# First modulation vectors of a diffusion step: weights as the stationary operand, the two conditions as moving columns

## Chip, cores and metric

The kernel runs on one core of one Trainium2 chip. Its time is the device time of one execution in microseconds (us); less is better.

## What is computed

The reference is one inference step of a two-layer backbone for two request groups, 1,024 latent tokens and 128 prompt tokens of width 1,024, in float32. In each layer a condition vector gives six modulation vectors, which scale, shift and gate the tokens' normed values. Only the first two of layer 0, the shift and the scale ahead of its first mixer, are touched here:

```python
def ada_modulation(cond, w_ada, b_ada):
    m = jax.nn.silu(cond) @ w_ada + b_ada
    return jnp.split(m[:, None, :], N_ADA, axis=-1)

def modulate(x, norm_w, shift, scale):
    return rms_norm(x, norm_w) * (1 + scale) + shift
...
sh1_p, sc1_p, g1_p, ... = ada_modulation(c_ctx[None, :], ada_w[i], ada_b[i])
sh1_s, sc1_s, g1_s, ... = ada_modulation(c, ada_w[i], ada_b[i])
hp = modulate(xp, norm_mix[i], sh1_p, sc1_p)
hs = modulate(xs, norm_mix[i], sh1_s, sc1_s)
```

There are two conditions, one for each group. For these two vectors the product is [2 x 1024] by [1024 x 2048], that is 8 MB of float32 weights for 2 rows of data. What follows them is the projection of the modulated tokens with `win0`.

## The kernel before, in words

Activations lie transposed: channels on the 128 partitions, tokens along the free axis, 1,152 tokens in three chunks of 384. `x` is eight tiles (KD = 8) of 128 channels each. A modulation vector is wanted the same way, as a column of 128 channels for each of 8 tiles and 2 conditions; it is kept in `ada`.

The opening (lines 505 to 524) runs so. The program loads chunk 0 of `x` and takes its norm (`norm_stats`, L260): ACT squares eight tiles, DVE adds the even ones and POOL the odd ones (L271), DVE joins the two (L272), a matmul with `ones` (L274) sums over channels, and `rsqrt` (L251) follows on DVE and ACT. Then come `ada_mat(1)` (scale) and `ada_mat(0)` (shift), then four weight tiles of `win0`, each split into a high and a low part (`wsplit`, L156: ACT L160, DVE L161), then for each chunk `norm_apply` (L278): DVE multiplies by the scale (`ht`, L289), ACT adds the shift and rounds (`hh`, L290 and L292), DVE forms the remainder (`hl`, L294 and L296). The projection (`mm3`, L330) multiplies with three matmuls for each weight tile (L335 to L337) and is the first large product. A small transpose of the conditions (`ps_sil`, L519) and a cast of `sel8` (L517) for later stages stand at the end of the opening.

`ada_mat` for one part loads eight tiles of 128 x 1,024 weights (512 KB each), tile k holding input channels 128k to 128k + 127. For each it makes two products: the stationary operand is `sil`, 128 channels by 2 conditions; the moving operand is 512 columns of the weights. The result is two rows of 1,024. ACT copies them out of PSUM (`arow`, L228), eight transposes turn them into columns (L231), and `ada_bias` (L207) adds the bias on DVE (L210) and, for the scale, joins it with the norm's weights (L214).

Buffers of `S` (L55) are handed out by age: the slot that has been free longest comes first. `x`, the norm's buffer `nt`, the weight tiles `wadan`, `arow`, `hh`, `hl` and `ht` all take theirs from it, so an `nt` or `ht` often gets a slot in which a weight tile lay, and has to wait until TensorE has read that tile. In the kernel before, `nt` of chunk 1 gets the slot of the third tile of part 0, and `nt` of chunk 2 that of the eighth.

The order on each engine isn't that of the text: a scheduler of the language places the instructions of all engines by its own estimate of their times, and each engine then runs its own list strictly in order. All loads are issued on SP's queue.

Of the kernel before, what the change touches and what calls it, by code (L numbers as in the profile page):

```python
# [17 lines left out]
P = 128  # L18
D = 1024
KD = 8  # L20
# [70 lines left out]
def hybrid_kernel(ctx: ExitStack, tc: tile.TileContext, I, O):  # L91
    nc = tc.nc
# [7 lines left out]
    S = Slots(spool, NSLOT)  # L100
# [5 lines left out]
    def PS(name, tag="pa"):  # L106
        return psum.tile([P, 512], F32, tag=tag, name=name, bufs={"pa": 3, "pb": 3, "pc": 2}[tag])
# [4 lines left out]
    def dma(out, in_):  # L112
        nc.sync.dma_start(out.bitcast(F32) if out.dtype == F32R else out,
                          in_.bitcast(F32) if in_.dtype == F32R else in_)
# [27 lines left out]
    ident = cst.tile([P, P], F32, name="ident")  # L142
# [13 lines left out]
    def wsplit(src, e=0):  # L156
        r = W("wr")
        dma(r, src)
        hi, lo = W("wh"), W("wl")
        nc.scalar.copy(hi, r)  # L160
        (nc.gpsimd if e else nc.vector).tensor_sub(lo, r, hi)  # L161
        return hi, lo

    def wtile(w, n=8, width=P):
        return [(w[0][:, k * width:(k + 1) * width], w[1][:, k * width:(k + 1) * width]) for k in range(n)]
# [5 lines left out]
    sil = cst.tile([P, 2 * KD], F32, name="sil")  # L171
# [35 lines left out]
    def ada_bias(layer, part, src):  # L207
        a = ada[layer][:, 8 * part:8 * part + 8, :]
        b0 = VEC[f"bada{layer}"][0] + 8 * part
        nc.vector.tensor_add(a, src, vec[:, b0:b0 + 8].unsqueeze(2).to_broadcast([P, 8, 2]))  # L210
        if part in (1, 4):
            n0 = VEC[("nmix" if part == 1 else "nmlp") + str(layer)][0]
            nb = vec[:, n0:n0 + 8].unsqueeze(2).to_broadcast([P, 8, 2])
            nc.vector.scalar_tensor_tensor(a, a, 1.0, nb, op0=ALU.add, op1=ALU.mult)  # L214

    def ada_mat(part):
        ps = [PS("ps_a", "pc") for _ in range(2)]
        for k in range(KD):
            r = S.alloc("wadan")
            dma(r[:, :D], I["wada0"][part, k])  # L220
            for q in range(2):
                nc.tensor.matmul(ps[q][0:2], sil[:, 2 * k:2 * k + 2], r[:, q * 512:q * 512 + 512],
                                 start=k == 0, stop=k == KD - 1)
            S.free(r)
            yield
        row = S.alloc("arow")
        for q in range(2):
            nc.scalar.copy(row[0:2, q * 512:q * 512 + 512], ps[q][0:2])  # L228
        pt = PS("ps_at", "pb")
        for k in range(KD):  # L230
            nc.tensor.transpose(pt[:, 2 * k:2 * k + 2], row[0:2, k * P:k * P + P], ident[0:2, 0:2])  # L231
        S.free(row)
        ada_bias(0, part, pt[:, 0:16].rearrange("p (k i) -> p k i", i=2))
        yield

    bg = []
# [268 lines left out]
    load_x(0)  # L505
    stats = [norm_stats(x, 0)]
    run(ada_mat(1))
    run(ada_mat(0))
    ws = [wtile(wsplit(I["win0"][4 + g])) for g in range(4)]
    hh, hl = alloc_h()  # L510
# [7 lines left out]
    pt = PS("ps_sil", "pb")  # L518
# [22 lines left out]
    for ch in range(NCH):  # L541
        c0 = ch * CH
        for g in range(4):
            ps = PS("ps_i")[:, :CH]
# [72 lines left out]
    for m in (2, 3, 0, 1):  # L617
        w = wtile(wsplit(I["win0"][m]))
        for ch in range(NCH):
            ps = PS("ps_i")[:, :CH]  # L620
# [83 lines left out]
    for ch in range(NCH + 1):  # L704
# [4 lines left out]
        for t in range(4):  # L709
            ps = PS("ps_k")[:, :n]  # L710
# [464 lines left out]
    r, vr = S.alloc("ctx"), S.alloc("ctxv")  # L1175
# [20 lines left out]
    for g in range(4):  # L1196
# [8 lines left out]
        for t, ch in order:  # L1205
# [3 lines left out]
            ps = PS("ps_n1")[:, :CH]  # L1209
# [9 lines left out]
        for ch in range(NCH):  # L1219
            for t in range(4):  # L1220
                wn = "naq" if t < 2 else "nak"
                pp_ = pq if t < 2 else pk
                ps = PS("ps_b", "pb")[:, :CH]
# [230 lines left out]
def tile_w(w, cols=None):  # L1454
    k, m = w.shape
    return np.ascontiguousarray(w.reshape(k // P, P, m // P, P).transpose(2, 1, 0, 3)).reshape(m // P, P, k)


def layout(a):
    r = {}  # L1460
# [4 lines left out]
    def put(name, v):  # L1465
        o, w = VEC[name]
        vec[:, o:o + w] = v
# [3 lines left out]
    for i in range(2):  # L1471
        put(f"bada{i}", cols(a[f"b_ada_l{i}"]))
        put(f"nmix{i}", cols(a[f"norm_mix_l{i}"]))
        put(f"nmlp{i}", cols(a[f"norm_mlp_l{i}"]))
        w = np.asarray(a[f"w_ada_l{i}"])
        if i == 0:
            r["wada0"] = np.ascontiguousarray(w[:, :2 * D].reshape(KD, P, 2, D).transpose(2, 0, 1, 3))
            r["wada0t"] = np.ascontiguousarray(w[:, 2 * D:].T).reshape(32, P, D)
        else:
            r["wada1"] = np.ascontiguousarray(w.T).reshape(48, P, D)  # L1480
        r[f"w1_{i}"] = tile_w(a[f"w_mlp1_l{i}"])
        w2 = np.asarray(a[f"w_mlp2_l{i}"]).reshape(2, 8, 2, P, 4, 256)
        r[f"w2_{i}"] = np.ascontiguousarray(w2.transpose(1, 4, 3, 2, 0, 5)).reshape(8, 4, P, 1024)
# [5 lines left out]
    w = np.asarray(a["w_in_l0"])  # L1489
# [3 lines left out]
    w = np.asarray(a["w_q_up_l0"]).reshape(256, 8, 96)  # L1493
    r["wqup"] = np.concatenate([w[:, :, :64].reshape(256, 512), w[:, :, 64:].reshape(256, 256),
                                w[:, :, 64:][:, :, swap].reshape(256, 256)], axis=1).reshape(2, P, 1024)
    w = np.asarray(a["w_kv_up_l0"]).reshape(P, 8, 128)
    r["wkvup"] = np.concatenate([w[:, :, :64].reshape(P, 512), w[:, :, 64:].reshape(P, 512)], axis=1)
    w = np.asarray(a["w_pool_l0"]).transpose(1, 0, 2).reshape(P, 512)
    r["wpool"] = np.concatenate([w, np.zeros_like(w)], axis=1)
    for i in range(2):  # L1500
        w = np.asarray(a[f"w_out_l{i}"]).reshape(2, 4, P, 4, 2, P)
# [29 lines left out]
    for g in range(4):  # L1531
        w, h = 2 << g, 1 << g
        e[g, :h] = w / (np.arange(h) + h)
        e[g, 16 - h:] = w / np.minimum(np.arange(h, 0, -1) + h, w)
    w = np.asarray(a["w_in_l1"])
# [49 lines left out]
```

## Time and profile before

| | us |
|---|---|
| median of 3 runs (3025.92 to 3040.58) | 3026.92 |
| the profiled execution, device time | 3023.98 |
| its span in the profile | 3022.2 |
| first product of `ada_mat` starts | 11.92 |
| first matmul of the projection starts | 47.43 |

The profile is of one execution. Times in its rows are microseconds from the span's start; L222 is line 222 of the kernel. PE is TensorE's matmul, PEld its weight load (they overlap), DVE, ACT and POOL are the vector, scalar and GpSimd engines, SPq is the queue that issues loads. `out<-in` names the tiles, the number after x counts the records, and brackets give the idle time before them and what ended it. A form such as `128*2 128x512` is that of the array (rows by columns of the stationary operand) and of the data. The granted clock (PEclk) is 1.00 at full speed.

### The profile page before, as it was taken

The page shows a single profiled execution, that of the slowest core. Times are in us where ns is not written, and L with a number is a line of the kernel's source. Part 1 is how long each engine was busy: PE and PEld are TensorE (multiplying, and loading weights), DVE is VectorE, ACT ScalarE, POOL GpSimd, SP SyncE. Part 2 cuts the span into 40 slices and gives each one's busy share as a digit, 9 for nine tenths or more (in the row PEclk, how much of TensorE's full clock was granted, in tenths as well). Part 3 has the DMA queues.
Part 4 walks back from the last instruction along what each step waited for, and adds up shares of the span by engine and source line. Part 5 has one row for each costly group of instructions (what it writes and reads, how often), then busy time and mean ns, then how long its engine had stood idle before and what let it go on. Part 6 is the DMA issues. An engine that isn't in the chain of part 4 may idle for free.

```text
span 3022.2 us, 46490 instructions
## 1 busy us (share of the span) xinstructions
PE 2910.4 (96%) x18302; PEld 2611.2 (86%) x18302; DVE 2160.5 (71%) x3921; ACT 1330.5 (44%) x2177; POOL 312.7 (10%) x210
## 2 busy tenths in 40 slices
PE   7998999889999999999999999998989999999999
PEld 4956666689999999999988888665889999999999
DVE  5977343797668889777789533677687678777765
ACT  5364344243436543453634522443244355453432
POOL 2004000143000020000221000000030000110000
PEclk9996999999999999999999999998999999999999
DMA  6529331432322334322556537796303232332322
GB/s 234 168 64 318 86 77 44 129 119 77 101 81 92 105 119 154 91 84 84 171 162 214 178 129 194 198 240 165 108 28 99 78 98 84 116 99 78 98 78 87
DMA packets 148268, 372.37 MB, mean 123 GB/s; under 512 B 14225, under 2 KB 67073, under 8 KB 148050
## 3 DMA queue, kind: packets, MB, share of 16 engines
q1 hardware_dynamic: 148050, 369.40, 40.0%
q8 instruction: 144, 2.36, 0.3%
q14 instruction: 74, 0.61, 0.1%
HBM read 310.69 MB, written 57.47 MB: 122 GB/s over the span
## 4 chain that ended last, share of the span: by engine, by line
PE 84%; DVE 6%; DMA 6%; issue 2%; ACT 1%; POOL 1%; SPq 0%; DVEq 0%; POOLq 0%; ACTq 0%
PE ps L452 9%; PE ps L454 9%; PE ps L453 9%; PE ps L422 8%; PE ps L424 8%; PE ps L423 8%; PE ps_pv L1077 4%; PE ps_n L335 2%; PE ps_n L336 2%; PE ps_n L337 2%; DVE trash L200 1%; PE ps_pv L1330 1%; PE ps_v L1354 1%; PE ps_v L1356 1%; PE ps_v L1355 1%
## 5 line engine op out<-in xcount | busy, mean ns | idle before, releaser
L452 PE MATMUL ps<-ml,wh 128*128 128x288 f32 x2048 | 591.9, 295 | 10.3 <-DVE ml L441 7.8
L453 PE MATMUL ps<-mh,wl 128*128 128x288 f32 x2048 | 600.8, 295 | 0.0
L454 PE MATMUL ps<-mh,wh 128*128 128x288 f32 x2048 | 596.6, 295 | 0.0
L422 PE MATMUL ps<-bl,wh 128*128 128x288 f32 x1792 | 532.9, 298 | 13.4 <-DVE bl L353 10.2
L423 PE MATMUL ps<-bh,wl 128*128 128x288 f32 x1792 | 529.7, 296 | 0.0
L424 PE MATMUL ps<-bh,wh 128*128 128x288 f32 x1792 | 528.2, 295 | 0.0
L452 PEld LDWEIGHTS ps<-ml,wh 128*128 128x128 f32 x2048 | 381.2, 188 | 11.3 <-DVE ml L441 8.3
L453 PEld LDWEIGHTS ps<-mh,wl 128*128 128x128 f32 x2048 | 385.1, 188 | 0.0
L454 PEld LDWEIGHTS ps<-mh,wh 128*128 128x128 f32 x2048 | 383.2, 188 | 0.1
L458 DVE SCALAR_TENSOR_TENSOR x<-ps,ada,x 128x288 f32<-128x288 f32 (+2 forms) x640 | 270.1, 451 | 119.1 <-PE ps L454 117.6
L422 PEld LDWEIGHTS ps<-bl,wh 128*128 128x128 f32 x1792 | 336.9, 188 | 16.7 <-issue 11.5
L424 PEld LDWEIGHTS ps<-bh,wh 128*128 128x128 f32 x1792 | 338.4, 189 | 0.0
L423 PEld LDWEIGHTS ps<-bh,wl 128*128 128x128 f32 x1792 | 337.6, 188 | 0.2
L395 ACT CAST wh<-s 128x512 fp32r<-128x512 f32 x256 | 146.1, 618 | 307.0 <-PE ps L454 216.7
L160 ACT CAST wh<-wr 128x1024 fp32r<-128x1024 f32 x188 | 196.9, 1049 | 165.7 <-PE ps L424 79.9
L200 DVE CUSTOM_DVE_ANT_0 trash<-wada,silu 128x1024 bf16<-128x1024 f32 x160 | 217.1, 1357 | 18.2 <-DMA wada<-in_wada 7.6
L161 DVE TENSOR_TENSOR wl<-wr,wh 128x1024 fp32r<-128x1024 f32 x144 | 179.6, 1251 | 44.3 <-ACT wh L160 44.3
L395 ACT CAST wh<-wr 128x1024 fp32r<-128x1024 f32 (+1 forms) x128 | 107.0, 836 | 220.0 <-PE ps L454 155.5
L161 POOL TENSOR_TENSOR wl<-wr,wh 128x1024 fp32r<-128x1024 f32 x44 | 122.2, 2784 | 708.7 <-ACT wh L160 687.4
L1035 DVE TENSOR_REDUCE stat<-ps_m 128x1 f32<-128x384 f32 x192 | 98.3, 552 | 117.0 <-PE ps_m L1034 116.7
L396 DVE TENSOR_TENSOR wl<-s,wh 128x512 fp32r<-128x512 f32 x232 | 157.6, 711 | 5.1 <-ACT wh L395 2.8
L1279 DVE CUSTOM_DVE_ANT_0 trash<-ps_m,ta 128x512 bf16<-128x512 f32 (+1 forms) x128 | 83.5, 652 | 98.1 <-PE ps_m L1277 90.4
(315 smaller groups left out, 6113.8 us busy)
## 6 DMA issues: line engine op xcount, KB each, us to landing
wr<-in_w SPq DMA_DIRECT2D x256, 512.0 KB
wada<-in_wada SPq DMA_DIRECT2D x48, 512.0 KB
wada<-in_wada0t SPq DMA_DIRECT2D x32, 512.0 KB
wr<-in_win SPq DMA_DIRECT2D x24, 512.0 KB
wr<-in_wout SPq DMA_DIRECT2D x24, 512.0 KB
vd<-vst SPq DMA_DIRECT2D x27, 384.0 KB
kk<-kd SPq DMA_DIRECT2D x32, 288.0 KB
nv<-vd SPq DMA_DIRECT2D x16, 576.0 KB
```

The costliest lines, as they stand in the source:

```text
L160: nc.scalar.copy(hi, r)
L161: (nc.gpsimd if e else nc.vector).tensor_sub(lo, r, hi)
L200: nc.vector.tensor_tensor_reduce(trash, r[:, :D], silu[i][:, :D], scale=1.0, scalar=0.0, op0=ALU.mult, op1=ALU.add, accum_out=a)
L395: nc.scalar.copy(h, src)
L396: (nc.gpsimd if j in EDGE and min(ps) in EDGE_POOL else nc.vector).tensor_sub(l, src, h)
L422: nc.tensor.matmul(ps, wh[:, a], hl[:, b], start=k == 0, stop=False)
L423: nc.tensor.matmul(ps, wl[:, a], hh[:, b], start=False, stop=False)
L424: nc.tensor.matmul(ps, wh[:, a], hh[:, b], start=False, stop=k == 3)
L452: nc.tensor.matmul(ps, wh, hl, start=kk == 0, stop=False)
L453: nc.tensor.matmul(ps, wl, hh, start=False, stop=False)
L454: nc.tensor.matmul(ps, wh, hh, start=False, stop=kk == 3)
L458: nc.vector.scalar_tensor_tensor(x[m][:, a:b], ps[:, a - ch * HC:b - ch * HC], g, x[m][:, a:b], op0=ALU.mult, op1=ALU.add)
```

## The change

The operands of the product swap their places. The weights are stored in another order: tile m of a part now holds output channels 128m to 128m + 127, and within it eight blocks of 128 input channels by 128 output channels. Each block is a stationary operand, and the two columns of `sil` for its input channels are the moving operand. Eight such products add up to two columns of the result, which stand in PSUM as they are wanted. The copies to `arow` and the transposes fall away, and `ada_bias` reads PSUM directly. The number, size and order of the loads stay the same.

```diff
     def ada_mat(part):
-        ps = [PS("ps_a", "pc") for _ in range(2)]
-        for k in range(KD):
+        ps = PS("ps_a", "pc")
+        for m in range(KD):
             r = S.alloc("wadan")
-            dma(r[:, :D], I["wada0"][part, k])
-            for q in range(2):
-                nc.tensor.matmul(ps[q][0:2], sil[:, 2 * k:2 * k + 2], r[:, q * 512:q * 512 + 512],
+            dma(r[:, :D], I["wada0"][part, m])
+            for k in range(KD):
+                nc.tensor.matmul(ps[:, 2 * m:2 * m + 2], r[:, k * P:k * P + P], sil[:, 2 * k:2 * k + 2],
                                  start=k == 0, stop=k == KD - 1)
             S.free(r)
             yield
-        row = S.alloc("arow")
-        for q in range(2):
-            nc.scalar.copy(row[0:2, q * 512:q * 512 + 512], ps[q][0:2])
-        pt = PS("ps_at", "pb")
-        for k in range(KD):
-            nc.tensor.transpose(pt[:, 2 * k:2 * k + 2], row[0:2, k * P:k * P + P], ident[0:2, 0:2])
-        S.free(row)
-        ada_bias(0, part, pt[:, 0:16].rearrange("p (k i) -> p k i", i=2))
+        ada_bias(0, part, ps[:, 0:16].rearrange("p (k i) -> p k i", i=2))
         yield
...
-            r["wada0"] = np.ascontiguousarray(w[:, :2 * D].reshape(KD, P, 2, D).transpose(2, 0, 1, 3))
+            r["wada0"] = np.ascontiguousarray(w[:, :2 * D].reshape(KD, P, 2, KD, P).transpose(2, 3, 1, 0, 4)).reshape(2, KD, P, D)
```

From line 225 on the changed kernel's lines are seven lower (L267 there is L274 here, L328 is L335). With `arow` gone, the slots move on: `nt` of chunk 1 now gets the slot of the second tile of part 0, and `nt` of chunk 2 that of the seventh. The scheduler also places the work around the product otherwise. Three places show it.

On TensorE, where the product ends and the projection begins, the kernel before has (`wadan_42` is the last weight tile, `ps_n_336` the norm of chunk 1):

```order
L222 MATMUL ps_a_187<-wadan_42_217,sil_83 2x512
L222 MATMUL ps_a_188<-wadan_42_217,sil_83 2x512
L231 MATMUL ps_at_224<-ident_75,arow_44_221 128x2 x8
L274 MATMUL ps_n_336<-nt_71_314,ones_74 128x384
L335 MATMUL ps_i_501<-hl0_54_266,wh_236 128x384
L336 MATMUL ps_i_501<-hh0_46_258,wl_237 128x384
L337 MATMUL ps_i_501<-hh0_46_258,wh_236 128x384
```

The changed kernel has there (`ps_n_406` and `ps_n_476` are the norms of chunks 1 and 2):

```order
L222 MATMUL ps_a_222<-sil_83,wadan_38_283 128x2 x8
L222 MATMUL ps_a_222<-sil_83,wadan_40_293 128x2 x8
L267 MATMUL ps_n_406<-nt_67_384,ones_74 128x384
L267 MATMUL ps_n_476<-nt_77_454,ones_74 128x384
L512 MATMUL ps_sil_543<-ident_75,sil_83 16x128
L328 MATMUL ps_i_571<-hl0_50_336,wh_306 128x384
L329 MATMUL ps_i_571<-hh0_42_328,wl_307 128x384
```

The norm of chunk 2 and the small transpose, which stood some 80 rows further on, inside the projection, now stand ahead of its first matmul.

On DVE, around the addition of the bias to the shift (L210), the kernel before has (`nt_71` is chunk 1's norm, `nt_81` chunk 2's):

```order
L271 TENSOR_TENSOR nt_71_314<-nt_71_314,sq_329 128x384
L210 TENSOR_TENSOR ada0_91<-ps_at_224,vec_73 128x16
L272 TENSOR_TENSOR nt_71_314<-nt_71_314 128x384
L271 TENSOR_TENSOR nt_81_384<-nt_81_384,sq_387 128x384
L294 SCALAR_TENSOR_TENSOR hl0_54_266<-ht_62_274,ada0_91,hh0_46_258 128x384
L252 TENSOR_SCALAR nt_71_314<-ps_n_336 128x384
```

The changed kernel has there (`nt_67` is chunk 1's norm, `nt_77` chunk 2's):

```order
L265 TENSOR_TENSOR nt_67_384<-nt_67_384 128x384
L264 TENSOR_TENSOR nt_77_454<-nt_77_454,sq_457 128x384
L264 TENSOR_TENSOR nt_77_454<-nt_77_454,sq_463 128x384
L264 TENSOR_TENSOR nt_77_454<-nt_77_454,sq_469 128x384
L210 TENSOR_TENSOR ada0_91<-ps_a_222,vec_73 128x16
L265 TENSOR_TENSOR nt_77_454<-nt_77_454 128x384
L287 SCALAR_TENSOR_TENSOR hl0_50_336<-ht_58_344,ada0_91,hh0_42_328 128x384
```

The whole addition for chunk 2, which takes in POOL's half at L265, now stands ahead of the first `hl`.

On ACT, after the casts of the first `win0` tiles, the kernel before has:

```order
L160 CAST wh_248<-wr_246 128x1024
L267 ACTIVATE nt_71_314<-x0_1_93 128x384
L267 ACTIVATE nt_71_314<-x1_2_94 128x384
L270 ACTIVATE sq_317<-x2_3_95 128x384
L270 ACTIVATE sq_320<-x3_4_96 128x384
```

The changed kernel has there:

```order
L160 CAST wh_318<-wr_316 128x1024
L263 ACTIVATE sq_387<-x2_3_95 128x384
L263 ACTIVATE sq_390<-x3_4_96 128x384
L263 ACTIVATE sq_393<-x4_5_97 128x384
L263 ACTIVATE sq_396<-x5_6_98 128x384
L263 ACTIVATE sq_399<-x6_7_99 128x384
L510 CAST sel8r_77<-sel8_76 128x48
L260 ACTIVATE nt_67_384<-x0_1_93 128x384
L260 ACTIVATE nt_67_384<-x1_2_94 128x384
```

The first two squares of chunk 1, which go into `nt` itself, moved behind five others and behind the cast of `sel8`, which stood far behind them before.

## The prediction

> **What bounds the kernel now.** The page comes first: its span, its busy times and its chain.
>
> ```profile
> span 3022.2 us, 46490 instructions
> ...
> PE 2910.4 (96%) x18302; PEld 2611.2 (86%) x18302; DVE 2160.5 (71%) x3921; ACT 1330.5 (44%) x2177; POOL 312.7 (10%) x210
> ...
> PE 84%; DVE 6%; DMA 6%; issue 2%; ACT 1%; POOL 1%; SPq 0%; DVEq 0%; POOLq 0%; ACTq 0%
> ```
>
> TensorE is on 84% of the chain that ended last, so time that is added on TensorE is kernel time wherever TensorE does not wait afterwards. The change touches only the opening; the second view is therefore busy time by stretch (columns: busy us and instructions of PE, PEld, DVE, ACT, POOL, then granted clock, DMA share, GB/s).
>
> ```profile
> 11.92:15.94 4.02, 4.02 (x5) 0.84 (x6) 0.56 (x1) 0.00 (x0) 0.33 (x1) 1.00 1.02 419
> 15.94:43.20 27.26, 27.26 (x70) 5.49 (x68) 10.92 (x18) 9.43 (x16) 4.54 (x3) 1.00 1.04 392
> 43.20:46.66 3.46, 1.04 (x10) 0.87 (x10) 2.55 (x5) 3.38 (x8) 2.43 (x3) 1.00 0.90 365
> 46.66:50.08 3.42, 3.42 (x10) 2.75 (x10) 2.86 (x7) 3.42 (x8) 0.00 (x0) 0.50 0.04 12
> ...
> 67.40:155.00 87.60, 87.60 (x493) 85.74 (x494) 81.61 (x171) 36.79 (x81) 1.06 (x1) 1.00 0.49 155
> 155.00:225.00 70.00, 70.00 (x285) 38.04 (x284) 49.37 (x102) 48.07 (x111) 4.03 (x2) 1.00 0.18 56
> 225.00:268.00 43.00, 32.50 (x97) 24.22 (x97) 34.30 (x68) 18.16 (x20) 33.72 (x21) 0.53 0.88 329
> ```
>
> From 11.92 to 43.2 us TensorE never idles: the modulation product owns it. From 67.4 to 225 us it never idles either (87.60 of 87.60, 70.00 of 70.00). Whatever delays the first input projection is therefore carried through to 225 us unshortened. Then come waits (32.50 of 43.00).
>
> The third view is the opening in order of time, which gives the hand-over to the projection (L335).
>
> ```profile
> 11.92 3.57 PE L222 MATMUL ps_a<-wadan,sil 128*2 128x512 f32 x4 [11.92 <-DMA wadan<-in_wada]
> ...
> 15.43 1.15 PE L274 MATMUL ps_n<-nt,ones 128*128 128x384 f32 x2
> ...
> 16.51 12.18 PE L222 MATMUL ps_a<-wadan,sil 128*2 128x512 f32 x28
> ...
> 36.44 0.94 ACT L267 ACTIVATE nt<-x 128x384 f32<-128x384 f32 x2 [0.53 <-PE ps_a L222]
> ...
> 44.32 0.41 PE L231 MATMUL ps_at<-ident,arow 2*128 2x2 f32 x4 [0.71 <-ACT arow L228]
> 44.86 0.16 DVE L210 TENSOR_TENSOR ada<-ps_at,vec 128x16 f32<-128x16 f32 x1
> ...
> 45.82 0.56 DVE L272 TENSOR_TENSOR nt<-nt 128x384 f32<-128x384 f32 x1 [0.80 <-POOL nt L271]
> ...
> 46.44 1.46 PE L274 MATMUL ps_n<-nt,ones 128*128 128x384 f32 x2 [1.71 <-DVE nt L272]
> ...
> 47.43 0.79 PE L335 MATMUL ps_i<-hl,wh 128*128 128x384 f32 x1
> ...
> 48.02 0.33 PEld L337 LDWEIGHTS ps_i<-hh,wh 128*128 128x128 f32 x1
> ...
> 52.08 3.62 POOL L271 TENSOR_TENSOR nt<-nt,sq 128x384 f32<-128x384 f32 x3 [6.29 <-ACT sq L270]
> ...
> 62.69 0.81 PE L274 MATMUL ps_n<-nt,ones 128*128 128x384 f32 x2
> ...
> 67.36 0.44 PE L335 MATMUL ps_i<-hl,wh 128*128 128x384 f32 x1 [0.97 <-ACT ain L551]
> ```
>
> The projection starts at 47.43 us. That instant is the quantity to forecast.
>
> **What goes.** The rows of one tile give the removed products.
>
> ```profile
> L222 PEld LDWEIGHTS ps_a<-wadan,sil x64: 80/85/127, 11.9 to 42.3; 128*2 128x2 f32 x64
> L222 PE MATMUL ps_a<-wadan,sil x64: 591/592/1057, 11.9 to 42.7; 128*2 128x512 f32 x64
> ```
>
> 32 instructions show as 64 records, so each float32 product is two load-and-stream passes. 28 of them take 12.18 us, counting 0.16 us of overhang (592 less one step): 0.43 us each, 64 x 0.43 = 27.5 us at full clock. The weights stream; the loads of two columns hide beneath. Also gone are the copies (L228) and transposes (L231) after the last product. That product starts at 42.7 and streams 0.43 us, so from about 43.1 to the addition at 44.86 us the path spends 1.75 us on them.
>
> **What comes.** 128 products, so 256 records, each loading 128 columns and streaming two. Streaming two columns is nearly nothing; loading becomes the work. No row of before has such a pair without transposing; the nearest are these.
>
> ```profile
> L712 PEld LDWEIGHTS ps_k<-small,wkf x8: 186/188/189, 173.3 to 177.2; 128*128 128x128 f32 x8
> ...
> 173.31 0.30 PEld L712 LDWEIGHTS ps_k<-small,wkf 128*128 128x128 f32 x2 [0.65 <-issue]
> 33.33 0.32 PEld L231 LDWEIGHTS ps_at<-ident,arow 2*128 2x128 f32 x4 [0.86 <-issue]
> L231 PEld LDWEIGHTS ps_at<-ident,arow x16: 133/136/138, 28.6 to 44.5; 2*128 2x128 f32 x16
> L231 PE MATMUL ps_at<-ident,arow x16: 195/197/218, 28.6 to 44.5; 2*128 2x2 f32 x16
> ```
>
> At L712 (plain float32, 128 columns, full clock) two loads take 0.30 us and one 0.188, so the second follows 0.11 us behind. By columns: (188 - 85) ns / 126 = 0.82 ns each, 105 ns for 128. At half clock the same load shows 0.33 us (L337 at 48.02, in the stretch with clock 0.50) and the two-column load 127 ns (the first of L222): (330 - 127) / 126 = 1.61 ns, 0.21 us for 128. So the new product costs 256 x 0.105 = 26.9 us at full clock, a wash against 27.5, but 256 x 0.21 = 53.8 us at half clock. The low end is L231's step, 0.062 us (0.32 less 0.133, over three): 16 us. The high end is a load and its matmul one after the other, 0.33 + 0.20 us: 136 us. I take 0.21: L712 has the new operand's type and shape, and L231 is a transpose.
>
> The Trainium skill ("TensorE: Matmul & The Clock Gate", LDWEIGHTS) gives a load as columns over 1.2, 107 ns for 128, with no word on the clock. By it the product would take 27.3 us at either clock, which also ends in the first rival below; the trace agrees at full clock (0.11 us) and disagrees at half clock (0.33 against 0.188 us per load).
>
> **Which clock.** TensorE is granted full clock only for some kinds of work.
>
> ```profile
> 234.40:241.22 6.82, 6.82 (x24) 5.21 (x24) 6.01 (x15) 4.09 (x4) 6.82 (x3) 0.50 0.92 370
> 241.22:248.05 6.83, 6.83 (x24) 5.37 (x23) 6.01 (x14) 3.05 (x4) 6.83 (x5) 0.50 1.02 403
> L682 PEld LDWEIGHTS ps_b<-rkh,bcs x28: 280/283/326, 230.3 to 249.5; 8*128 8x128 f32 x28
> ```
>
> Here TensorE is busy in 6.82 of 6.82 us, loads in 5.21, and still has 0.50: its matmuls use 8 of 128 rows. Being occupied, and loading weights, does not by itself raise the clock. The new product streams 2 columns of each 128 it loads, and begins, as now, at half clock (its first load takes 127 ns, later ones 85). I expect it to stay there to its end. What these rows cannot exclude is that loads with all 128 rows count.
>
> The Trainium skill (same page, Part 1) lets the clock rise after about 3.4 us of sustained activity. If loads count as activity it would rise here too, and the time is that of the first rival below.
>
> **The sum.** First tile from 11.92: 16 x 0.21 = 3.4, to 15.3; the norm's pair (1.15) to 16.5; 240 x 0.21 = 50.4, to 66.9 us. The 16 transfers keep their number, size and place in SP's queue; a tile lands in 1.3 us (512 KB at 392 to 419 GB/s) and is used in 3.4, so DMA stays ahead.
>
> Two things stand between that and L335 (the changed kernel's L328). First, buffers rotate by age, and the norm's buffer of token chunk 2 is now the one of the seventh tile of the second part, free at 66.9 - 3.4 = 63.5; today's wait of that kind is the 0.53 us at 36.44. (Chunk 1 has the second tile's, free near 46.5, and is done long before.) Then 0.94 on ACT, 3.6 on POOL (L271) and 0.56 on DVE: 68.6. Second, TensorE's order now has the norm pairs of chunks 1 and 2 ahead of the projection, and DVE's has the chunk 2 addition ahead of the first hl. All projection matmuls queue behind that pair. It starts at about 68.7, and L335 followed such a pair by 0.99 us: 69.7, with the small transpose 69.8. That is 69.8 - 47.43 = 22.4 us late.
>
> Back come the pair that now sits inside the projection at 62.69 (0.65 us of streaming) and perhaps the 0.97 us at 67.36, because chunk 2 is ready early: 0.7 to 1.6. Half clock lasts some 3 us into the projection in both. Net +21 to +22; I take +22. The copies and transposes are covered by the norm chain, so their 1.75 us are not counted again. The reordered waits from 225 us on (10.5 us idle) can move a few us either way.
>
> The profiled execution took 3023.98 us (span 3022.2 and 1.8 around), so 3046. The median of the runs, 3026.92, is 2.9 higher: the forecast is 3026.9 + 22 = 3049 us.
>
> **The rivals.** *Full clock (not slower).* If loads with 128 rows raise the clock after the start, the product ends at 16.5 + 240 x 0.105 = 41.7 us, 1.4 us earlier than now. The projection does not follow, for ACT now has the cast of sel ahead of chunk 1's squares.
>
> ```profile
> 39.60 0.33 SPq L113 DMA_DIRECT2D sel<-in_sel  x1
> ...
> GB/s 0 123 246 182 323 303 365 401 418 412 431 404 415 407 404 415 407 410 415 404 415 407 379 371 375 376 372 352 314 382 369 22 11 5 0 5 0 0 79 270
> ```
>
> That transfer is third from the end of a queue which runs (slices of 1.5 us) until about 46 us; it lands near 43.5. Then 0.94, two chunks on POOL (7.2), 0.56 and 1.0: L335 at 53.3, +5.8, less 1.3: about +4.5, 3031 us. For it: loads at L712 overlap cleanly, and nothing shows 128-row loads alone. Against: the 8-row stage. It decides if the mean load is under about 0.15 us. Chance 0.23. A load at the transposes' 0.062 us ends the same way.
>
> *Loads that do not overlap.* Each record 0.53 us: product until 149, about +100, 3130 us. Against: L231's four pairs take 0.41 us together. Chance 0.03.
>
> *The change gains.* The product ends early as in the first rival, and the new order also removes the idle time after 225 us: at most 10.5 + 5, about 3011. Nothing asks for it. Chance 0.03.
>
> **How the numbers follow.** Half clock has 0.71, and its own range is 3041 to 3060 (load steps of 0.19 to 0.24 us are -5 and +7, the later waits the rest). The range 3027 to 3060 adds the full-clock case and leaves out some 0.15. A measurement tells about 0.5%, 15 us, from no change: slower takes half clock but for its lowest 0.03, and the serial case, 0.71; within 0.5% the full-clock case and that remainder, 0.26; faster 0.03.
>
> **What would show it.** L222 with 256 loads of mean near 0.33 us, running from 11.9 to about 67; granted clock 0.50 for that stretch; L335 (seven lines higher there) first near 70; the stretch after it as long as now, to 225 us. Loads of 0.19 us and a product done by 43 would prove the clock argument wrong; a pair of chunk 2 that does not end last before the projection, the order argument; a gain or loss of over 5 us after 225 us, the claim that the delay is simply carried through.

## The result, and the profile after

| | before | changed |
|---|---|---|
| median of four runs each, us | 3028.56 | 3071.19 |
| lowest and highest, us | 3025.92, 3040.58 | 3065.69, 3076.20 |
| ratio, 95% interval | | 1.0133 [1.0114, 1.0151] |
| profiled execution, span, us | 3022.2 | 3073.9 |

The changed kernel is 43 us slower where 22 were forecast. All times in this document are of runs at the usual clock; one run of a kernel below (the old product in the new order, 3665.55 us at a mean granted clock of 0.716) is left out. The page of the changed kernel, its span, busy times and chain:

```profile
span 3073.9 us, 46836 instructions
...
PE 2956.6 (96%) x18478; PEld 2672.9 (87%) x18478; DVE 2163.2 (70%) x3921; ACT 1329.4 (43%) x2173; POOL 312.5 (10%) x210
...
PE 85%; DVE 6%; DMA 5%; ACT 1%; issue 1%; POOL 1%; SPq 1%; DVEq 0%; POOLq 0%; ACTq 0%
```

TensorE is busy 46 us longer (2956.6 for 2910.4), no other engine over 3. The opening is as forecast. The rows of the weight tiles (nanoseconds minimum, median, maximum; first and last start):

```profile
L222 PEld LDWEIGHTS ps_a<-sil,wadan x256: 288/333/337, 11.4 to 67.1; 128*128 128x128 f32 x128
L222 PE MATMUL ps_a<-sil,wadan x256: 212/352/353, 11.4 to 67.1; 128*128 128x2 f32 x128
```

And the opening of the changed kernel in order of time:

```profile
16.28 51.20 PE L222 MATMUL ps_a<-sil,wadan 128*128 128x2 f32 x240
...
64.10 0.94 ACT L260 ACTIVATE nt<-x 128x384 f32<-128x384 f32 x2 [11.93 <-PE ps_a L222]
...
65.11 3.53 POOL L264 TENSOR_TENSOR nt<-nt,sq 128x384 f32<-128x384 f32 x3 [13.52 <-ACT nt L260]
...
68.68 0.56 DVE L265 TENSOR_TENSOR nt<-nt 128x384 f32<-128x384 f32 x1 [0.80 <-POOL nt L264]
...
69.29 1.65 PE L267 MATMUL ps_n<-nt,ones 128*128 128x384 f32 x2 [0.33 <-DVE nt L265]
...
70.80 0.67 PE L328 MATMUL ps_i<-hl,wh 128*128 128x384 f32 x1
```

240 records in 51.20 us are 0.213 us each, the median load takes 0.333 us (the shortest 0.288), and the projection starts at 70.80 us, 23.4 later than before. The norm steps of chunk 2 and its pair on TensorE end last, in the order that was foretold.

Where the rest comes from shows when the starts of equal matmuls in the two traces are set against each other (times here and in the table are those of the kernel before). The delay is 22.8 us at 155, 27.6 at 175, 23.1 at 1,000, 22.7 at 1,724 and 24.1 at 1,858 us: but for some 5 us that come between 155 and 175 us and are given back by 1,000, it is carried through for 1,800 us. Then it grows to 51.0 us at 2,145 us and stays there to the end. That stretch is the neighbourhood attention of layer 1. Its row of the windows in the kernel before (columns as in the prediction):

```profile
1858.00:2145.00 287.00, 263.64 (x1091) 176.97 (x1090) 199.42 (x498) 125.67 (x268) 16.58 (x7) 0.93 0.80 205
```

The same work in the changed kernel:

```profile
1882.00:2196.00 314.00, 284.59 (x1091) 190.52 (x1090) 201.30 (x498) 126.11 (x268) 16.55 (x7) 0.85 0.73 188
```

The same 1,091 matmul records, 27 us longer, at a granted clock of 0.85 for 0.93. Either the new order of instructions costs there, or the clock differs between any two runs, or both.

### The profile page after: what moved, and what is told of

Same layout as the page of the kernel before. It is cut to its first block, busy times and chain, and to the rows that moved or that the text cites. A ratio compares the mean times of both kernels' runs of the same rounds, so it can differ in the third digit from the quotient of the medians.

```text
span 3073.9 us, 46836 instructions
## 1 busy us (share of the span) xinstructions
PE 2956.6 (96%) x18478; PEld 2672.9 (87%) x18478; DVE 2163.2 (70%) x3921; ACT 1329.4 (43%) x2173; POOL 312.5 (10%) x210
## 4 chain that ended last, share of the span: by engine, by line
PE 85%; DVE 6%; DMA 5%; ACT 1%; issue 1%; POOL 1%; SPq 1%; DVEq 0%; POOLq 0%; ACTq 0%
PE ps L445 9%; PE ps L447 9%; PE ps L446 9%; PE ps L415 8%; PE ps L417 7%; PE ps L416 7%; PE ps_pv L1070 4%; PE ps_n L328 2%; PE ps_n L330 2%; PE ps_n L329 2%; PE ps_pv L1323 2%; PE ps_a L222 2%; DVE trash L200 1%; PE ps_v L1347 1%; PE ps_o L328 1%; PE ps_o L329 1%
```

## The experiments

The scheduler orders every engine anew for each version of the program, so a piece of the change can't be undone without moving all that follows. Most kernels below therefore hold an order. Behind the traced program a function chains the instructions of each engine in a list taken from one of the two schedules. The edges set the order alone; nobody waits for them.

```diff
+def hold_order(tc):
...
+        for v in d:
+            k += v
+            if last is not None:
+                tc.add_manual_dep(pr[k], last.name, NOSYNC, reason="order")
+            last = pr[k]
...
         hybrid_kernel(tc, I, O)
+        hold_order(tc)
```

Where the new product runs in the old order, the slots also rotate as with `arow` (a slot is taken and given back in its place). "Above" is the median against that of the kernel before on the same chip. The table sets all profiled runs against the first profile of the kernel before: the delay of the first projection matmul (47.4 us there), of the first, the seven-eighths and the last matmul `ps_st<-q,k` of the neighbourhood attention (1,858, 2,103 and 2,145 us), and what the last column adds to the one ahead of it.

| kernel | order behind the opening, and in the neighbourhood attention | 47 | 1,858 | 2,103 | 2,145 | last eighth | above, us | ratio, 95% interval |
|---|---|---|---|---|---|---|---|---|
| changed | new, new | 23.4 | 24.1 | 45.6 | 51.0 | +5.4 | 42.6 | 1.0133 [1.0114, 1.0151] |
| changed, again | new, new | 23.9 | 26.0 | 37.0 | 43.1 | +6.1 | 37.9 | 1.0127 [1.0113, 1.0141] |
| new product | old, old | 22.8 | 23.5 | 26.1 | 27.2 | +1.1 | 22.1 | 1.0080 [1.0056, 1.0105] |
| new product | new, old | 24.0 | 28.9 | 32.3 | 33.5 | +1.2 | 29.9 | 1.0100 [1.0082, 1.0119] |
| new product | old, new | 22.4 | 26.3 | 33.3 | 39.0 | +5.7 | 38.4 | 1.0124 [1.0106, 1.0141] |
| old product | new, new | 19.9 | 24.8 | 21.0 | 27.2 | +6.2 | 18.6 | 1.0072 [1.0047, 1.0098] |
| old product, opening held | new, new | 12.7 | 21.3 | 24.1 | 30.3 | +6.2 | 27.6 | 1.0093 [1.0075, 1.0110] |
| old product | old, new | 0.1 | -0.8 | -8.2 | -2.0 | +6.2 | 8.6 | 1.0028 [1.0011, 1.0046] |
| kernel before, again | old, old | -1.3 | 1.9 | 8.5 | 9.8 | +1.3 | 3.0 | 1.0002 [0.9986, 1.0018] |
| half the contraction | old, old | -5.2 | 4.5 | 19.3 | 20.4 | +1.1 | 5.6 | 1.0021 [1.0003, 1.0039] |
| 64 columns | old, old | 23.6 | 25.3 | 38.3 | 40.0 | +1.7 | 25.2 | 1.0088 [1.0061, 1.0115] |
| 128 columns | old, old | -2.1 | -1.6 | 13.4 | 14.7 | +1.3 | 1.0 | 1.0017 [0.9999, 1.0035] |
| 128 columns, nothing held | a third | -2.3 | 1.9 | 9.3 | 10.8 | +1.5 | 5.5 | 1.0018 [1.0001, 1.0035] |
| changed, two SP rows back | new, new but SP | 24.6 | 35.3 | 38.2 | 46.4 | +8.2 | 44.3 | 1.0152 [1.0127, 1.0177] |
| changed, DVE back | new, new but DVE | 23.8 | 24.5 | 28.7 | 38.7 | +10.0 | 37.0 | 1.0133 [1.0106, 1.0160] |
| before, two SP rows forward | old, old but SP | 1.1 | 4.0 | 4.4 | 12.1 | +7.7 | 3.5 | 1.0017 [0.9999, 1.0036] |

### The new product in the old order

Edit: `hold_order` with the list of the kernel before, from the first projection matmul on.

> The new product (256 weight loads), with every instruction behind the opening, from the first projection matmul on, held on its engine in the order in which it stands in the kernel before; the slots rotate as there too. Theory O (the scheduler's new order in the neighbourhood attention of layer 1 costs what the opening does not explain): the opening still costs its +23 us, the +27 between 1,890 and 2,130 us are gone: 3052 us (3047 to 3057). Theory T (any shift of the same order by some 24 us loses that much there, since clock steps and transfers fall differently): as the changed kernel, 3066 to 3076. Theory C (the opening is the whole cause, and costs over 40): 3071 as well, with the first projection matmul at over 85 us.

22 us above, and the whole delay in the profile is the opening's 22.8 at the first projection matmul; 27.2 at the end. Theory C falls. Theory T falls as a mean (the same shift in the old order does not cost 40); O stands.

### The old product in the new order

Edit: the list of the changed kernel, under the old `ada_mat`.

> The old product (condition vectors stationary, 64 wide matmul records, row copies and transposes), with everything behind the opening held in the order of the changed kernel. Theory O: the opening is as before (first projection matmul near 47 us), the stretch 1,890 to 2,130 us is some 20 to 27 us longer: 3046 to 3056. Theory T and theory C: as the kernel before, 3025 to 3032.

19 us above, as O wants, but for another reason: this kernel's own opening came out 19.9 us longer. Its product's last matmul starts at 61.6 us for 42.7, with the fetches and norms standing for another opening. The reading is lost, and the stretch 1,858 to 2,145 us added only 2.4.

### Half of the contraction left out

```diff
-            for k in range(KD):
+            for k in range(KD // 2):
```

> As the new product in the old order, but with half of the contraction left out of the first modulation vectors (4 of 8 blocks, 128 weight loads for 256; all weights are still fetched). If the loads at 0.2135 us each are the cost of the opening, it is 27 us shorter, down to where the fetches or the norm end it: first projection matmul at 44 to 50 us, time 3025 to 3032. If something else ends the opening (the norm of the third chunk, the fetches), under 10 us go: over 3040.

The tile's rows in this kernel, with 128 loads for 256:

```profile
L226 PEld LDWEIGHTS ps_a<-sil,wadan x128: 288/333/337, 11.9 to 40.3; 128*128 128x128 f32 x128
L226 PE MATMUL ps_a<-sil,wadan x128: 213/353/353, 12.0 to 40.3; 128*128 128x2 f32 x128
```

Loads last as long as with 256, and half of them end 27 us sooner, so their number times 0.213 us is the opening's cost. But a projection that starts 5.2 us early wins nothing: TensorE then waits for ACT, and by 76 us the delay is 2.3. The time, 3037.84 us, is above the 3025 to 3032 expected, and the trace shows no more than that delay up to 300 us, for 5.6 us in the medians. Waits of this kernel between 42 and 80 us:

```profile
PE ps_i L336 <- ACT ain L552: 4.6, 2, 3.7
```

The 27 us of TensorE time bought 16.5 us in the medians (22.1 less 5.6).

### 64 columns, then 128, behind each load

The two columns are read over and over (a step of zero), and the results stand 64 or 128 columns apart. With 128 they need two PSUM banks and two small copies on DVE. The edit for 128 (the one for 64 repeats the pair 32 times for 64):

```diff
-                nc.tensor.matmul(ps[:, 2 * m:2 * m + 2], r[:, k * P:k * P + P], sil[:, 2 * k:2 * k + 2],
+                nc.tensor.matmul(ps[m // 4][:, m % 4 * P:m % 4 * P + P], r[:, k * P:k * P + P],
+                                 sil[:, 2 * k:2 * k + 2].unsqueeze(1).to_broadcast([P, 64, 2]),
```

> As the new product in the old order, but each load is followed by 64 columns (the two conditions repeated 32 times) where there were 2. Is the half clock of the opening the work's doing, because next to nothing streams? If so, 64 columns lift it: the load falls from 0.333 to 0.188 us, 256 steps of 0.11 to 0.16 us are 27 to 41 us, first projection matmul at 46 to 58 us, time 13 to 24 us below the new product in the old order. If the clock stays at half: either the columns hide behind the loads (no difference) or they add 0.107 us to each step, and it is up to 27 us slower.

> As the new product in the old order, with 128 columns behind each load for 2, so that streaming and loading would take the same time at either clock; two copies of the results on DVE come in. 64 columns left step and load at 0.2135 and 0.333 us. If the clock follows the time that the array streams: now it streams without a gap, the load falls to 0.188 us, 256 steps of 0.107 to 0.13 us are 27 to 33 us, the first projection matmul comes at 46 to 52 us and the time is 18 to 24 us below the new product in the old order. If something else holds the clock at half: steps of 0.2135 us, no difference.

The tile's rows with 64 columns:

```profile
L226 PEld LDWEIGHTS ps_a<-sil,wadan x256: 288/333/338, 12.3 to 68.0; 128*128 128x128 f32 x128
L226 PE MATMUL ps_a<-sil,wadan x256: 314/421/447, 12.4 to 68.1; 128*128 128x64 f32 x128
```

The same with 128 columns:

```profile
L227 PEld LDWEIGHTS ps_a<-sil,wadan x256: 190/191/338, 11.8 to 42.8; 128*128 128x128 f32 x128
L227 PE MATMUL ps_a<-sil,wadan x256: 273/273/553, 11.8 to 42.9; 128*128 128x128 f32 x128
```

64 columns hide behind loads of 0.333 us, and nothing changes. With 128, after a start at 0.338 us, the loads take 0.191, and all 256 records with the norm's pair between them end at 43 us. The projection then starts here:

```profile
45.34 0.44 PE L343 MATMUL ps_i<-hl,wh 128*128 128x384 f32 x1 [0.34 <-DVE hl L302]
```

That is 2.1 us earlier than in the kernel before, with 256 weight loads, and the time is that of the kernel before as far as can be told (1.0 us above in the medians, 0 to 11 by the interval). The half clock is the cause of the opening's cost, and it was the narrow stream of 2 or 64 columns behind each load that held it. Where between 64 and 128 columns the clock rises was not tried.

### The changed kernel again, and its order cut in two

Four kernels on one chip: the changed one; the old product with the opening held too; the changed one with the old order from the first local score matmul on; and the reverse.

> The changed kernel once more, on the chip of the next three. Single runs of one kernel spread over 20 us here, and nearly all of that arises in the neighbourhood attention of layer 1. Theory O (the new order costs there beyond the opening): again 36 to 46 us above the kernel before. Theory R (the first four runs lay high by chance, and only the opening counts): 20 to 28 us above it.

> The old product; the opening held in the order of the kernel before, its own matmuls, copies and fetches included (the earlier kernel with the new order left these free, and its opening came out 20 us longer), everything behind it in the order of the changed kernel. First projection matmul at 46 to 49 us in either case. Theory O: 13 to 22 us above the kernel before. Theory R: within 5 us of it.

> The changed kernel in its own order up to the first local score matmul of layer 1's neighbourhood attention (near 1,880 us), from there in the order of the kernel before. Theory O with the cost in that stage: 20 to 28 us above the kernel before, as the new product in the old order (+22). If the cost comes from the order ahead of that stage: as the changed kernel, 36 to 46 above.

> The reverse: the new product in the old order up to that matmul, from there in the order of the changed kernel. Theory O with the cost in that stage: 36 to 46 us above the kernel before. If the cost comes from the order ahead of it, or there is none: 20 to 28 us above.

The changed kernel lies 38 us above again, so theory R falls. With the new order until the neighbourhood attention and the old one in it, 30 remain; the reverse gives 38. If the new order costs anything by itself, then in that stage, by some 8 us, though the two intervals overlap. The old product with the opening held still started its projection 12.7 us late, against the expectation, so its 27.6 us can't be put down to the stage, of which the last eighth adds 6.2 in the profile.

Of some 1,500 DVE and 7,200 TensorE instructions from that stage on, 14 and 13 stand elsewhere, of ACT's 4 and of SP's 2; the first of them runs near 2,112 us in the kernel before. So what differs between 1,858 and 2,103 us is not the stage's order, and the last eighth holds all of it. The two runs of the changed kernel differ by 10.5 us there (21.5 and 11.0 between the columns 1,858 and 2,103), and all sixteen rows spread from -7.4 to +21.5, in both orders alike. The last eighth is sharp: 1.1 to 1.7 us with the old order or a third one, 5.4 to 6.2 in all six profiled runs with the new one.

### Which of the moved instructions

In the old order SP fetches the row of maxima (`q<-mrow`), which the local score matmuls of the last head take in, ahead of two fetches of attention output. In the kernel before, SP's queue:

```profile
2115.14 0.32 SPq L113 DMA_DIRECT2D od<-no  x1
2116.85 0.29 SPq L113 DMA_DIRECT2D mrow<-row  x1
2117.80 0.32 SPq L113 DMA_DIRECT2D op<-od  x1
2118.22 0.24 SPq L113 DMA_DIRECT2D q<-mrow  x1
2118.55 1.68 SPq L113 DMA_DIRECT2D op<-od  x2
```

In the changed kernel:

```profile
2162.37 0.39 SPq L113 DMA_DIRECT2D od<-no  x1
2163.47 0.28 SPq L113 DMA_DIRECT2D mrow<-row  x1
2163.85 4.13 SPq L113 DMA_DIRECT2D op<-od  x2
2168.03 0.28 SPq L113 DMA_DIRECT2D q<-mrow  x1
2168.36 0.81 SPq L113 DMA_DIRECT2D wr<-in_wout  x2
```

The two fetches of `op` ahead of `q<-mrow` keep the queue for 4.13 us, so `q<-mrow` is issued 4.56 us after the store of `mrow` for 1.37. That a fetch of `op` waits there for the store `od<-no` fits the rows (the single `op` of the old order is issued only 2.66 us behind it) but was not tried. TensorE's waits in the last eighth of the kernel before (us in total, times, longest):

```profile
PE ps_st L1294 <- DVE p L1324: 3.7, 4, 1.7
PE ps_st L1295 <- DMA op<-od: 1.6, 1, 1.6
```

And of the changed kernel:

```profile
PE ps_st L1288 <- DMA q<-mrow: 8.0, 1, 8.0
PE ps_st L1287 <- DVE p L1317: 1.8, 3, 0.9
```

Three kernels move these two rows, or DVE's fourteen, alone. The first edits SP in the changed kernel, the third does the reverse in the kernel before:

```diff
 mrow<-row
-op<-od
-op<-od
 q<-mrow
+op<-od
+op<-od
```

> The changed kernel in its own order, but for two rows of SP near the end of layer 1's neighbourhood attention: two fetches of attention output, op, that stand ahead of the fetch q<-mrow in the new order go back behind it, as they stand in the old. In nine profiled runs so far the last eighth of the local score matmuls took 41.6 to 43 us with the old order of that place and 47 to 48 with the new. Theory Q (score matmuls of the last heads wait for q, which waits behind op, which waits for data): PE's wait of 9 us there falls under 3, the last eighth to 41 to 44 us, the time 3 to 7 us below the changed kernel. Rival D (DVE's moved hi/lo splits of op hold up the last softmax): still 46 to 48 us, or longer.

> The changed kernel in its own order, but DVE from the first local score matmul on in the old one (14 instructions go back by some places, the splits of op behind the softmax subtractions). Rival D: the last eighth falls to 41 to 44 us. Theory Q: it stays at 45 to 48, since q is still fetched late.

> The kernel before, its order held on every engine, but for the same two fetches of op on SP, which go ahead of q<-mrow as in the changed kernel. Theory Q: the last eighth 45 to 49 us for 41.6, PE waits 7 to 10 us for the late q, time 3 to 7 us above the kernel before, which no more than five rounds can just tell. Rival D: as before.

Waits of the kernel before with the two rows forward:

```profile
PE ps_st L1302 <- DMA q<-mrow: 7.7, 1, 7.7
PE ps_st L1301 <- DVE p L1331: 3.3, 3, 1.7
```

The two SP rows alone put the wait of 8 us there and stretch the last eighth by 7.7 us: theory Q holds in this direction. In the other it doesn't: the last eighth, expected at 41 to 44 us, takes 49.7. In the changed kernel with its SP rows back, the wait for `q` is gone and another stands in its place:

```profile
PE ps_st L1292 <- DVE p L1322: 6.8, 4, 5.0
PE ps_st L1293 <- DMA op<-od: 4.3, 1, 4.3
```

DVE's own wait there says why:

```profile
DVE oh L895 <- DMA op<-od: 6.8, 1, 6.8
```

DVE's list has the split of `op` (L895) ahead of the subtraction that the last scores wait for, and `op` now lands later. With DVE back and SP as in the new order, TensorE waits 8.5 us at the same matmuls, and the last eighth is +10.0, so rival D falls as well. So the moves belong together. SP's alone in the old order lengthen the last eighth by 7.7 us, the new order with only SP's undone by 8.2, with only DVE's undone by 10.0; all of them together lengthen it by 5.4 to 6.2, against 1.1 to 1.7 without any.

### What stays of the rest

> The kernel before in its own order up to the first local score matmul of layer 1's neighbourhood attention, from there on all engines in the order of the changed kernel (33 instructions stand some places elsewhere). Theory O: the stage's order costs 9 to 15 us by itself, 3038 to 3045. Theory Q alone: only the 5 to 8 us of the last eighth, 3034 to 3038. Theory R (no order effect): 3026 to 3032. The last eighth of the local score matmuls takes 46 to 49 us in the first two, 42 in the third.

> The kernel before once more, for its profile. Its single runs lie between 3018 and 3042 us, the profiled one at 3024. Theory L (the clock in the neighbourhood attention of layer 1 differs from run to run): up to 1,858 us within 3 us of the first profile, and what the total differs arises between 1,858 and 2,145 us, with the granted clock of that stage lower where it is longer.

> The changed kernel with 128 columns behind each load and two small copies on DVE, in whatever order the scheduler gives it (a third one). Opening: first projection matmul at 44 to 50 us, as with the held order. Time 3026 to 3035 if this order does no harm later, up to 3048 if it holds such a piece as the changed kernel's does.

The new order of the stage by itself, under the old product, is 8.6 us above (ratio 1.0028 [1.0011, 1.0046], which is 3 to 14 us), with the last eighth at +6.2. That does not tell theory O's 9 us from theory Q's 5. That this profiled run is 1.3 us shorter than the first profile of the kernel before, in spite of it, shows how little one run says: it gained 7.4 us between 1,858 and 2,103. The stage in the second profile of the kernel before, an identical program:

```profile
1857.00:2153.00 296.00, 272.09 (x1103) 182.91 (x1103) 198.79 (x497) 126.11 (x268) 16.57 (x7) 0.89 0.78 201
```

(The window opens some 3 us ahead of the stage's first local score matmul, hence the 12 more records; from the first to the last of these matmuls the stage takes 295 us here and 287 in the first profile.) Within 2 us of the first up to 1,858, then 8 us longer at a clock of 0.89 for 0.93: theory L. The profile on which the prediction rests caught this stage on a good run. The widened product with nothing held is 5.5 us above the kernel before (ratio 1.0018 [1.0001, 1.0035]), in a third order with a last eighth of +1.5. No version beat the kernel before; the one with 128 columns in the old order can't be told from it.

## Why the prediction was wrong, point by point

**The opening bound and its removal: right.** 64 records of 0.43 us gave way to 256 of 0.213; leaving out half of them ended the product 27 us sooner.

**The half clock: right, and now shown.** Loads of 0.333 us to the last, as at L337 of the kernel before at clock 0.50. The clock column could not show it; the windows of the changed kernel have 1.00 there, although every load lasts as at half clock, so durations are the measure in the opening:

```profile
16.50:67.10 50.60, 50.60 (x238) 50.60 (x239) 17.79 (x24) 13.54 (x24) 5.44 (x7) 1.00 0.65 241
```

The first rival, full clock at 3031 us, did not occur. The kernels with 128 columns have full clock, and their 3030.26 and 3034.51 us lie near its price, but by luck: they run in other orders and start the projection at 45.3 and 45.2 us, where the rival, with the cast of `sel` ahead of chunk 1's squares, had it at 53.3. What was left open in the prediction (whether loads of 128 rows count) is settled for this case: 51 us of them without a gap, with 2 or 64 columns behind each, did not lift the clock. The Trainium skill ("TensorE: Matmul & The Clock Gate", Part 1) says that a monitor watches how busy TensorE is and releases the full clock after some 3.4 us of sustained activity. The trace disagrees as long as loads are taken for activity, and agrees if streaming is meant: with 128 columns the loads fall from 0.338 to 0.191 us.

**The chain of chunk 2 and the hand-over: right in its steps, but worth little.** Forecast 69.8 us, found 70.80; the ACT, POOL and DVE steps took 0.94, 3.53 and 0.56 us for the 0.94, 3.6 and 0.56 assumed. That chain ended last, but only just. In the new product in the old order, where chunk 2's pair isn't ahead of the projection, the first weight load of the projection waits for `hl`, and comes 0.6 us earlier:

```profile
70.23 0.29 PEld L336 LDWEIGHTS ps_i<-hl,wh 128*128 128x128 f32 x1 [2.33 <-DVE hl L295]
```

So the bias, `hh` and `hl` behind the product hold the projection nearly as long, and the reordering on which the prediction counted its delay costs 0.6 us. In the kernel before it was `hl` too, so the 0.99 us between the pair and L335 isn't the pair's:

```profile
47.43 0.29 PEld L335 LDWEIGHTS ps_i<-hl,wh 128*128 128x128 f32 x1 [0.67 <-DVE hl L294]
```

**What comes back: nearly right.** 0.7 to 1.6 us were to be regained; the delay went from 23.4 to 22.8. The half clock did not last equally long into the projection, as assumed: the projection's loads take 0.33 us until 71.59 and 0.19 from 71.91, so some 1 us of it in the changed kernel, against nearly 3 in the kernel before (47.43 to 50.08).

**The delay carried through, the later waits "a few us either way": this step failed.** The delay was to reach 225 us unshortened, and the reordered waits behind that were put at nothing net. Two things went otherwise. First, the delay rose from 22.8 us at 155 to 27.6 at 175: TensorE, which never idles there in the kernel before, waits 2.4 us for ACT there in the changed kernel (in the old order the new product's delay rises by 1.0). That was given back by 1,000 us. Second, behind 1,858 us the scheduler had moved 33 instructions nobody had looked at; the prediction took the change to touch only the opening. In the profiles these moves cost 4 to 5 us (1.1 to 1.7 against 5.4 to 6.2), in the medians 8.6 [3, 14] under the old product. The place could be seen: in the trace of before TensorE waits 1.6 us there for a fetch, with `op`, `q<-mrow` and `op` issued within a microsecond of each other, and the order of the changed kernel has `q<-mrow` behind both.

**The base: low by chance.** The sum was made on a profile of 3023.98 us and a median of three runs of 3026.92; larger groups of runs of the kernel before have medians from 3027.3 to 3032.2.

**The sum.** Opening 22.1 us (interval 17 to 32, the new product in the old order) and the stage's order 8.6 (3 to 14) are 31, for 38 to 43 found. The intervals hold the difference of 7 to 12 us between them, but no run shows what it consists of. One thing on record bears on it: every run lists its mean granted clock, and in 90 runs of the kernel before the time goes with it (3034.8 us in the mean for the 22 at 0.968 or less, 3022.6 for the 23 at 0.972 or more; a straight line through all falls by 2.2 us for each 0.001). The changed kernel's two groups average 0.967 and 0.968, the new product in the old order 0.971, the 90 runs 0.970. Brought to one clock by that line, as an estimate, the opening costs 28 us (the delay in the trace is 22.8) and the stage's order 5, which is 33 for 32 to 34 found. Whether the new order lowers the clock, the longer waits do, or the runs fell that way by chance stays open. The order ahead of the neighbourhood attention does not show it: the delay at 1,858 us was 24.1, 26.0 and 28.9 with it, 23.5 and 26.3 without. The changed kernel with its SP rows back lost 11 us more than the changed kernel before 1,858 us, with equal order until far behind that; this stays open too.

## What to carry to other kernels

A stationary operand that is used for two columns costs a load per 128 columns at whatever clock the array is granted, and such a stream did not earn full clock; streaming as many columns as are loaded brought the same 256 loads to full clock, and to no more time than the old product took. Where a scheduler places the whole program anew, compare the order to the very end, above all what now stands ahead of a small fetch in a queue, and price each such place from the waits of the trace. And before a total from one profile is explained to the microsecond, learn from a second one of the same program which stage differs by itself.

## What the runs showed of the hardware that was not expected

- 128-column float32 loads in a row lasted 0.333 us with 2 or 64 columns behind each, over 51 us without a gap, and 0.191 us with 128 columns; the step fell from 0.213 to under 0.12 us (31 us for 256).
- 64 columns behind a load add nothing to its step of 0.213 us.
- In 90 runs of one program, at mean granted clocks of 0.965 to 0.975, the time rose as the clock fell, by 2.2 us for each 0.001 (a straight line through the runs).
- One program's neighbourhood attention took 287 and 295 us in two runs at granted clocks of 0.93 and 0.89; over the profiled runs of all kernels its part up to 2,103 us spread by 29 us. The Trainium skill ("TensorE: Matmul & The Clock Gate", Part 1) has the monitor's window run free of the program, so that equal kernels meet it at different phases; these two runs agree with that, though no run here shows the window itself.
- Two fetches of 576 KB ahead of one of 4 KB in SP's queue issued it 3.2 us later (4.56 for 1.37 us behind the store that it reads), and TensorE's wait grew from 1.6 to 8.0 us.
